# An encoder layer in float32 on one core: up products in twos, a first group of three, diagonals without a split, and smaller stores at the end

## The chip, the cores and the metric

The kernel runs on one core of a Trainium2 chip. A core has a matrix engine (TensorE, PE in the profile, with its weight loads shown as PEld), a vector engine (VectorE, DVE), an activation engine (ScalarE, ACT), a general engine (GpSimd, POOL), and a sync engine (SyncE, SP) whose queue issues most of the transfers; 16 DMA engines carry them. Each engine runs its own instructions in order and waits on semaphores for the others. The metric is the device time of one execution in microseconds (us); the time of a kernel is the median of its runs.

## The reference

One layer of an encoder, on 512 tokens of 2048 channels, all in float32 and with one output:

```python
xn = rms_norm(x, attn_norm_g)
u_val, u_gate, q, k, v = split(xn @ w_in)            # 2048 -> 5 x 1024
y_conv = silu(layer_norm(dwconv31(u_val * sigmoid(u_gate))))
y_na = neighbourhood_attention(q, k, v, rpb)         # 16 heads of 64, 8x64 grid
mixed = concat(rms_norm(y_conv), rms_norm(y_na))
x = x + mixed @ w_out                                # 2048 -> 2048
xn = rms_norm(x, ffn_norm_g)
gate, val = split(dwconv3(xn @ w_up))                # 2048 -> 2 x 5632
x = x + (silu(gate) * val) @ w_down                  # 5632 -> 2048
out = rms_norm(x, final_norm_g)
```

A root-mean-square norm divides each token's vector by the root of its mean square. The factor belongs to a token, so it may be applied after a product with the weights; the kernel does that.

## The kernel before

**Data.** Activations lie transposed: a tile has 128 channels as partitions and the 512 tokens as columns. Weights come from memory in units of 128 x 1024 (512 KB) into a ring of 7 buffers named `raw`.

**Products of float32 made of parts.** Each weight unit is split in two by `parts` (L113-118): ACT makes the rounded part `whi` (L116), DVE the remainder `wlo` (L117); each has 4 buffers. Activations are split likewise. `mm3` (L124-129) adds three matmuls to a bank of PSUM: high by high (L127), high by low (L128), low by high (L129). The list `plan` holds the units in order; `weights()` hands out the next one and makes units up to 3 ahead (`AHEAD`).

**Order.** The kernel is written against a tile framework that orders the instructions of an engine by its own estimate of when they are due, within the data dependences, so that work stands elsewhere in an engine's queue than the source's order says. Work beside the main loop is written as generators in the lists `steps` and `asteps`; `tick` (called after each product) runs one step of the first generator of each and ties what it issues behind the last matmul of that product. A `yield` in such a generator so puts off its rest by one product.

**The per-token factor.** `rsqrt_steps` (L179-213) makes 1/sqrt(mean + eps) for each token. With the sum of squares over channels in `acc`, matmuls with a column of ones (L190) put the tokens on the partitions, 128 x 4 values; L192 and `root` (L172-177: a square root on ACT, then a reciprocal and one correction step on DVE) work on those. To get the factor back as a row per token and the same on every partition, the kernel makes diagonal matrices of it and multiplies them by ones: the 128 x 4 factor is split into a rounded part (L197) and the rest (L198), each is spread on four diagonals side by side (`dg`, 128 x 512, L202), and two matmuls (L208) add them up; ACT copies the result from PSUM (L212). It is called six times: for the norm before the input projection (about 45 us into the span), for the layer norm of the convolution, for the two group norms (the convolution's, `ra`, near 497 us), for the norm before the feed-forward part (`rstd2`, near 683 to 694 us) and for the final one (`rstd3`, near 2010 us).

**The output projection** is made in two halves of 16 products; its first half begins before `ra` exists, and `read_a` then takes each bank with L586 (product by `ra`) and L587 (sum into `x2`). Its banks come from `psm`, a pool of three banks of PSUM with the tag "mm".

**The feed-forward part.** The up product is made with seven products instead of eight half-size ones (a scheme of Strassen's kind). For each of the 44 values of f (128 gate and 128 value channels) `factors` (L655-681) forms the seven weight units out of four loaded ones by sums on DVE (L666, L668, L673, L677), and `combine` and `halves` (L597-635) have formed the seven combinations of activations once, each of 256 columns and split (L600 on ACT, L601 on DVE), laid side by side as one 512-column tile: high in the left half, low in the right.

`up` (from f = 4, L708-769) makes a product c of eight channel tiles k: a *wide* matmul (L716) takes `whi` by both halves of the tile, 512 columns; a *low* one (L721) takes `wlo` by the left half, 256 columns, and adds to the bank's right half. A product is seven wide, eight low, and the last wide. After it ACT copies the bank's halves out (`vv`, `pl`, L728), and DVE sums the seven results into gate and value.

`up_apart` (f = 0 to 3, L771-809) works with three 256-column matmuls per k (`mm3`) and banks of 256 columns, copied by L800 and L803. For f = 0, `first_two` (L789) interleaves the first two products: both run their first seven k and then their last, since the last tile of the combinations comes late.

The product c = 6 has the bank "po", all others take the three "mm" banks in turn.

`hidden` (L821) applies the token factor, the convolution of width 3 and the gate; `down` (L836) multiplies four hidden tiles by the down weights (`pd`), ACT copies the bank (L847), and POOL issues a DMA that adds it to the residual in memory (L848). The down products of one group of four f run between the up products of the next (`between`).

**The tail.** The last down products and the final norm: 384 tokens are handled by channel, 128 by token. `finish` (L902) scales a pair of 128 x 384 tiles, on DVE (L912) or for every third pair on ACT and POOL (L909, L910), and stores the pair by one DMA (L916); the first pair is stored by two DMAs of one tile each (L914). `spread` (L933) runs between the last matmuls and calls the second half of `rsqrt_steps` at the step (g, k) = (1, 1), then one `finish` at each later step. Stores go by SP's queue, in order. The last token block follows with four stores (L975).

Of the kernel before, what the change touches and what calls it, by code (L numbers as in the profile page):

```python
# [67 lines left out]
def layer(ctx: ExitStack, tc: tile.TileContext, xT, xG, w_in, w_v, w_out, w_up, w_down, par, tab, g3, out, last_out):  # L68
# [110 lines left out]
    def rsqrt_steps(acc, n, name, to=slice(0, S), keep=True, by_token=None, free=False, rest=1):  # L179

        def bank():
            if free:
                return psa.tile([P, 2, S], F32, tag="sc", name="st")[:, 0]
            return psa.tile([P, S], F32, tag="po", name="st")

        m = (to.stop - to.start) // P
        ps = bank()[:, :m]
        v, r, y = (sm.tile([P, S // P], F32, tag="rs" + c, name="rs" + c)[:, :m] for c in "vry")
        for i in range(m):
            nc.tensor.matmul(ps[:, i:i + 1], acc[:, to.start + i * P:to.start + (i + 1) * P], ones[:, 0:1],  # L190
                             start=True, stop=True)
        nc.vector.tensor_scalar(v, ps, 1.0 / n, EPS, op0=ALU.mult, op1=ALU.add)  # L192
        root(r, y, v)
        if by_token is not None:
            by_token.append(y)
        yh, yl = (sm.tile([P, S // P], dt, tag="rs" + c, name="rs" + c)[:, :m] for c, dt in (("h", F32R), ("l", F32)))
        nc.vector.tensor_copy(yh, y)  # L197
        nc.vector.tensor_sub(yl, y, yh.bitcast(F32))  # L198
        ds = []
        for part in (yh.bitcast(F32), yl):  # L200
            ds.append(t2("dg", F32R)[:, :m * P])
            nc.vector.tensor_mul(ds[-1].rearrange("p (i k) -> p i k", k=P), ident.unsqueeze(1).broadcast_to([P, m, P]),  # L202
                                 part.unsqueeze(2).broadcast_to([P, m, P]))
        for _ in range(rest):
            yield
        ps = bank()[:, :m * P]
        for i, dg in enumerate(ds):
            nc.tensor.matmul(ps, ones_r, dg, start=i == 0, stop=i == 1)  # L208
        if not keep:
            return ps  # L210
        res = t2(name)
        nc.scalar.activation(res, ps, AF.Copy)  # L212
        return res
# [431 lines left out]
    def stats2():  # L645
        acc2, q = t2("acc2"), t2("sq")
        nc.sync.dma_start(acc2, sq2[0])
        nc.sync.dma_start(q, sq2[1])
        yield
        nc.vector.tensor_add(acc2, acc2, q)  # L650
        yield
        yield
        rstd2.append((yield from rsqrt_steps(acc2, D, "rstd2", free=True, rest=2)))
# [53 lines left out]

    def up(f, between):  # L708

        def product(c):  # L710

            w = weights()
            ps = (psa.tile([P, S], F32, tag="po", name="pu") if c == 6 else
                  psm.tile([P, S], F32, tag="mm", name="pu"))
            def wide(k):
                return nc.tensor.matmul(ps, w[0][:, k * P:(k + 1) * P], comb[c][k], start=k == 0, stop=k == U - 1)  # L716

            for k in range(U - 1):
                wide(k)
            for k in range(U):  # L720
                nc.tensor.matmul(ps[:, H:], w[1][:, k * P:(k + 1) * P], comb[c][k][:, :H], start=False, stop=False)  # L721
            i = wide(U - 1)
            tick(i)
            between(c)
            return ps[:, :H], ps[:, H:]

        def copy(to, ps):
            nc.scalar.activation(to, ps, AF.Copy)  # L728

        def pair(name):  # L730
            return t2(name).rearrange("p (i t) -> p i t", i=2)

        def both(x):
            return x.unsqueeze(1).broadcast_to([P, 2, H])


        vv, low = pair("vv"), pair("pl")
        for i in range(2):
            m, l = product(i)
            copy(vv[:, i], m)  # L740
            copy(low[:, i], l)
        m7, l = product(2)
        add(vv, vv, low)
        low = pair("pl")
        copy(low[:, 0], l)
        m1, l = product(3)
        copy(low[:, 1], l)
        uu, v = pair("uu"), pair("vl")
        u, u2 = uu[:, 0], uu[:, 1]
        add(u2, m7, low[:, 0])  # L750
        add(v, vv, both(u2))
        m6, l = product(4)
        add(u, m1, low[:, 1])
        low = pair("pl")
        copy(low[:, 0], l)
        add(u2, u, m6)
        m2, l = product(5)
        add(u2, u2, low[:, 0])
        add(v, v, both(u2))
        add(vv[:, 1], vv[:, 1], u2)  # L760
        low, g = pair("pl"), pair("g")
        copy(low[:, 0], l)
        add(g[:, 0], u, m2)
        m3, l = product(6)
        copy(low[:, 1], l)
        add(g[:, 1], vv[:, 1], m3)
        add(g, g, low)
        g, v = (t.rearrange("p i t -> p (i t)") for t in (g, v))
        return g, v

    def up_apart(f, between):  # L771

        def begin(c):
            return weights(), (psa.tile([P, S], F32, tag="po", name="pu") if c == 6 else
                               psm.tile([P, S], F32, tag="mm", name="pu"))[:, :H]

        def part(c, w, ps, ks):
            for k in ks:
                m = comb[c][k]
                i = mm3(ps, w, k, m[:, :H], m[:, H:], k == 0, k == U - 1)  # L780
            return i

        def product(c):
            w, ps = begin(c)
            tick(part(c, w, ps, range(U)))
            between(c)
            return ps

        def first_two():  # L789
            got = [begin(c) for c in range(2)]  # L790
            for c in range(2):
                tick(part(c, *got[c], range(U - 1)))
            for c in range(2):
                part(c, *got[c], range(U - 1, U))
            return [ps for _, ps in got]

        vv, v, uu, g = (t2(n).rearrange("p (i t) -> p i t", i=2) for n in ("vv", "vl", "uu", "g"))
        both = lambda x: x.unsqueeze(1).broadcast_to([P, 2, H])
        for i, ps in enumerate(first_two() if f == 0 else map(product, range(2))):
            nc.scalar.activation(vv[:, i], ps, AF.Copy)  # L800
        u, u2 = uu[:, 0], uu[:, 1]
        add(v, vv, both(product(2)))
        nc.scalar.activation(u, product(3), AF.Copy)  # L803
        add(u2, u, product(4))
        add(v, v, both(u2))
        add(vv[:, 1], vv[:, 1], u2)
        add(g[:, 0], u, product(5))
        add(g[:, 1], vv[:, 1], product(6))
        return tuple(t.rearrange("p i t -> p (i t)") for t in (g, v))
# [123 lines left out]
    def spread(g, k):  # L933
        if (g, k) == (0, 1):
            next(stats)
        elif (g, k) == (1, 1):
            try:
                next(stats)
            except StopIteration as e:
# [3 lines left out]
            nc.scalar.activation(rb[1], rb[0], AF.Copy)  # L943
        elif rb and pairs:
            at = pairs.pop(0)
            finish(at, rb[at % 3 == 1], at % 3 == 1)

    for g, ps in enumerate(banks):
        for i in range(CH):
# [100 lines left out]
```

## Time and profile before

| | |
|---|---|
| median of 3 runs | 2035.49 us (2032.01 to 2036.54) |
| the profiled execution | 2032.23 us |
| its span, first to last instruction | 2030.3 us |
| PE busy | 2016.6 us, 99% of the span |
| DVE, ACT, POOL busy | 1673.5, 1045.7, 159.7 us |
| mean granted TensorE clock | 0.998 of full speed |
| DMA | 276.4 MB, 136 GB/s on average |

The rows shown below are of these kinds. A row of the busy times has an engine, its busy time, the share of the span and the count of instructions. The chain is the work that ended last, followed back: start (us), length (us), engine, name of the result and line. A group's row has line, engine, operation, result and operands, shapes, count, then busy time and the mean of one (ns), then the idle time of the engine ahead of it and what ended it. A row of PE's waits has the waiting matmul, what released it, and total, count and longest wait in us. A timeline row has start, length, engine and line, with neighbours of one kind merged (x2); a matmul's length there covers its whole way through the engine, and the distance of two starts is what one costs. A row of GB/s gives the DMA rate in 40 equal slices of its window.

### The profile page before, as it was taken

What the parts mean: (1) busy time and instruction counts of PE and PEld (TensorE: products, weight loads), DVE (VectorE), ACT (ScalarE), POOL (GpSimd) and SP (SyncE); (2) the same over time, 40 slices, a digit from 0 to 9 for tenths busy, and PEclk for the clock granted to TensorE, in tenths of its full rate; (3) what the DMA queues carried; (4) which work ended last, traced back from release to release, by engine and by line L of the source; (5) the groups of instructions that cost most, each with busy time, mean ns of one, the idle gap of its engine ahead of it and who ended that gap; (6) DMA issues with size and microseconds to landing.
All of it is one profiled execution on the core that took longest, in us unless ns stands there. A gap on an engine that the chain in (4) does not pass through costs nothing.

```text
span 2030.3 us, 28220 instructions
## 1 busy us (share of the span) xinstructions
PE 2016.6 (99%) x10672; PEld 1726.0 (85%) x10672; DVE 1673.5 (82%) x2293; ACT 1045.7 (52%) x1674; POOL 159.7 (8%) x188
## 2 busy tenths in 40 slices
PE   9999999999999999999999999999999999999998
PEld 7888888888888998888888888888888888888887
DVE  7986888988577898888888888788888888889875
ACT  7323344466346555554555555555555555555563
POOL 0000000000001001111111111111111111110111
PEclk9999999999999999999999999999999999999999
DMA  7232333346347436566565565555565565564583
GB/s 256 83 104 86 115 96 109 104 131 212 104 124 177 124 105 145 127 144 146 125 146 146 135 136 146 134 136 145 125 145 146 125 146 145 130 141 126 145 212 120
DMA packets 97207, 276.40 MB, mean 136 GB/s; under 512 B 10928, under 2 KB 11696, under 8 KB 97072
## 3 DMA queue, kind: packets, MB, share of 16 engines
q1 hardware_dynamic: 71712, 228.45, 36.6%
q0 software_dynamic: 25216, 46.15, 15.4%
q8 instruction: 84, 1.38, 0.3%
q14 instruction: 51, 0.42, 0.1%
q10 hardware_dynamic: 144, 0.01, 0.0%
HBM read 220.04 MB, written 54.53 MB: 135 GB/s over the span
## 4 chain that ended last, share of the span: by engine, by line
PE 97%; DVE 2%; issue 0%; ACT 0%; DMA 0%; ACTq 0%; DVEq 0%
PE pu L716 25%; PE pu L721 13%; PE pd L129 8%; PE pd L127 8%; PE pd L128 8%; PE pj L127 6%; PE pj L129 5%; PE pj L128 5%; PE po L127 3%; PE po L128 3%; PE po L129 3%; PE pv L313 1%; PE pv L315 1%; PE pv L314 1%; PE pu L127 1%; PE pu L128 1%
## 5 line engine op out<-in xcount | busy, mean ns | idle before, releaser
L116 ACT ACTIVATE whi<-raw 128x1024 fp32r<-128x1024 f32 x364 | 384.8, 1058 | 481.8 <-PE pj L128 137.2
L117 DVE TENSOR_TENSOR wlo<-raw,whi 128x1024 fp32r<-128x1024 f32 x364 | 444.5, 1222 | 206.6 <-ACT whi L116 194.7
L716 PE MATMUL pu<-xc,whi 128*128 128x512 f32 x2240 | 574.5, 391 | 0.0
L716 PEld LDWEIGHTS pu<-xc,whi 128*128 128x128 f32 x2240 | 409.1, 189 | 73.7
L721 PEld LDWEIGHTS pu<-xc,wlo 128*128 128x128 f32 x2240 | 305.6, 190 | 21.9
L721 PE MATMUL pu<-xc,wlo 128*128 128x256 f32 x2240 | 312.3, 282 | 0.0
L128 PE MATMUL pd<-hl,whi 128*128 128x512 f32 x640 | 249.2, 389 | 0.0
L129 PE MATMUL pd<-hh,wlo 128*128 128x512 f32 x640 | 249.2, 391 | 0.0
L127 PE MATMUL pd<-hh,whi 128*128 128x512 f32 x640 | 249.0, 391 | 0.0
L848 POOL DMA_DIRECT2D x2d<-pdc x160 | 139.6, 874 | 1165.4 <-ACT pdc L847 952.4
L128 PE MATMUL pj<-xl,whi 128*128 128x512 f32 x512 | 200.1, 391 | 0.0
L129 PE MATMUL pj<-xh,wlo 128*128 128x512 f32 x512 | 199.8, 390 | 0.0
L127 PE MATMUL pj<-xh,whi 128*128 128x512 f32 x512 | 198.8, 393 | 0.0
L728 ACT ACTIVATE pl<-pu 128x256 f32<-128x256 f32 x280 | 104.5, 382 | 165.4 <-PE pu L716 165.2
L116 ACT ACTIVATE whi<-ws 128x1024 fp32r<-128x1024 f32 x132 | 139.8, 1059 | 80.0 <-PE pu L716 57.8
L117 DVE TENSOR_TENSOR wlo<-ws,whi 128x1024 fp32r<-128x1024 f32 x132 | 161.0, 1220 | 20.1 <-ACT whi L116 20.0
L367 DVE SCALAR_TENSOR_TENSOR y<-ch,prm,y 128x500 f32<-128x500 f32 (+14 forms) x240 | 173.5, 742 | 4.3
L129 PEld LDWEIGHTS pd<-hh,wlo 128*128 128x128 f32 x640 | 120.1, 188 | 28.8 <-DVE wlo L117 3.0
L128 PEld LDWEIGHTS pd<-hl,whi 128*128 128x128 f32 x640 | 120.3, 188 | 24.9
L127 PEld LDWEIGHTS pd<-hh,whi 128*128 128x128 f32 x640 | 120.5, 188 | 21.9
L847 ACT ACTIVATE pdc<-pd 128x512 f32<-128x512 f32 x160 | 93.8, 588 | 84.2 <-PE pd L129 84.1
L127 PEld LDWEIGHTS pj<-xh,whi 128*128 128x128 f32 x512 | 96.2, 188 | 20.4 <-issue 0.2
(206 smaller groups left out, 2887.3 us busy)
## 6 DMA issues: line engine op xcount, KB each, us to landing
raw<-in_w_up SPq DMA_DIRECT2D x176, 512.0 KB, 3.7
raw<-in_w_down SPq DMA_DIRECT2D x88, 512.0 KB, 4.0
x2d<-pdc POOLq DMA_DIRECT2D x160, 256.0 KB, 4.9
raw<-in_w_in SPq DMA_DIRECT2D x60, 512.0 KB, 3.8
raw<-in_w_out SPq DMA_DIRECT2D x32, 512.0 KB, 3.7
raw<-in_w_v SPq DMA_DIRECT2D x16, 512.0 KB, 4.1
tab<-in_tab SPq DMA_DIRECT2D x32, 256.0 KB, 5.0
x<-in_xG SPq DMA_DIRECT2D x16, 256.0 KB, 5.4
```

What stands on the lines that cost most here:

```text
L116: i = nc.scalar.activation(hi[:, :n], raw[:, :n], AF.Copy)
L117: j = nc.vector.tensor_sub(lo[:, :n], raw[:, :n], hi[:, :n].bitcast(F32))
L127: nc.tensor.matmul(ps, hi[:, a], mh, start=start, stop=False)
L128: nc.tensor.matmul(ps, hi[:, a], ml, start=False, stop=False)
L129: return nc.tensor.matmul(ps, lo[:, a], mh, start=False, stop=stop)
L313: nc.tensor.matmul(ps, xh, wh[:, f], start=kk == 0, stop=False)
L367: nc.vector.scalar_tensor_tensor(y[:, a:b], h[:, a + j - PAD:b + j - PAD], prm[:, o + j:o + j + 1], y[:, a:b], op0=ALU.mult, op1=ALU.add)
L716: return nc.tensor.matmul(ps, w[0][:, k * P:(k + 1) * P], comb[c][k], start=k == 0, stop=k == U - 1)
L721: nc.tensor.matmul(ps[:, H:], w[1][:, k * P:(k + 1) * P], comb[c][k][:, :H], start=False, stop=False)
L728: nc.scalar.activation(to, ps, AF.Copy)
L847: nc.scalar.activation(t, ps, AF.Copy)
L848: nc.gpsimd.dma_start(xd[d], t, accum_op=ALU.add)
```

## The change

It has four parts. *Diagonals*: in `rsqrt_steps` the cast, the subtraction and the spreading of the rest are replaced: the first diagonal (in the rounded type) is made from the factor itself, and the second, for each 128 columns, as identity times factor less the first diagonal, by one operation. *Twos*: in `up` the products (0,1), (2,3) and (4,5) share one block of low matmuls: eight wide of the first, one wide of the second (on its own bank), eight low of the first, eight low of the second, seven wide of the second. *Threes*: for f = 0 the first three products are interleaved, and `stats2` waits one product longer. *Stores*: `spread` takes up the factor one step earlier, and all pairs that DVE finishes are stored by two DMAs of one tile each.

```diff
@@ rsqrt_steps
-        yh, yl = (sm.tile([P, S // P], dt, tag="rs" + c, name="rs" + c)[:, :m] for c, dt in (("h", F32R), ("l", F32)))
-        nc.vector.tensor_copy(yh, y)
-        nc.vector.tensor_sub(yl, y, yh.bitcast(F32))
-        ds = []
-        for part in (yh.bitcast(F32), yl):
-            ds.append(t2("dg", F32R)[:, :m * P])
-            nc.vector.tensor_mul(ds[-1].rearrange("p (i k) -> p i k", k=P), ident.unsqueeze(1).broadcast_to([P, m, P]),
-                                 part.unsqueeze(2).broadcast_to([P, m, P]))
+        ds = [t2("dg", F32R)[:, :m * P] for _ in range(2)]
+        nc.vector.tensor_mul(ds[0].rearrange("p (i k) -> p i k", k=P), ident.unsqueeze(1).broadcast_to([P, m, P]),
+                             y.unsqueeze(2).broadcast_to([P, m, P]))
+        for i in range(m):
+            o = slice(i * P, (i + 1) * P)
+            nc.vector.scalar_tensor_tensor(ds[1][:, o], ident, y[:, i:i + 1], ds[0][:, o].bitcast(F32),
+                                           op0=ALU.mult, op1=ALU.subtract)
@@ stats2
         yield
+        yield
         nc.vector.tensor_add(acc2, acc2, q)
@@ up
+        opened = {}
+
+        def bank(c):
+            return (psa.tile([P, S], F32, tag="po", name="pu") if c == 6 else
+                    psm.tile([P, S], F32, tag="mm", name="pu"))
+
+        def wides(c, w, ps, ks, stop=False):
+            for k in ks:
+                i = nc.tensor.matmul(ps, w[0][:, k * P:(k + 1) * P], comb[c][k], start=k == 0,
+                                     stop=stop and k == ks[-1])
+            return i
+
+        def lows(c, w, ps, stop=False):
+            for k in range(U):
+                i = nc.tensor.matmul(ps[:, H:], w[1][:, k * P:(k + 1) * P], comb[c][k][:, :H], start=False,
+                                     stop=stop and k == U - 1)
+            return i
+
         def product(c):
             w = weights()
-            ps = (psa.tile([P, S], F32, tag="po", name="pu") if c == 6 else
-                  psm.tile([P, S], F32, tag="mm", name="pu"))
-            def wide(k):
-                return nc.tensor.matmul(ps, w[0][:, k * P:(k + 1) * P], comb[c][k], start=k == 0, stop=k == U - 1)
-
-            for k in range(U - 1):
-                wide(k)
-            for k in range(U):
-                nc.tensor.matmul(ps[:, H:], w[1][:, k * P:(k + 1) * P], comb[c][k][:, :H], start=False, stop=False)
-            i = wide(U - 1)
+            if c == 6:
+                ps = bank(c)
+                wides(c, w, ps, range(U - 1))
+                lows(c, w, ps)
+                i = wides(c, w, ps, range(U - 1, U), stop=True)
+            elif c % 2:
+                ps = opened.pop(c)
+                lows(c, w, ps)
+                i = wides(c, w, ps, range(1, U), stop=True)
+            else:
+                ps, opened[c + 1] = bank(c), bank(c + 1)
+                wides(c, w, ps, range(U))
+                wides(c + 1, made[weights.at], opened[c + 1], range(1))
+                i = lows(c, w, ps, stop=True)
             tick(i)
@@ up_apart
-        def first_two():
-            got = [begin(c) for c in range(2)]
-            for c in range(2):
+        def first_three():
+            got = [begin(c) for c in range(3)]
+            for c in range(3):
                 tick(part(c, *got[c], range(U - 1)))
-            for c in range(2):
+            for c in range(3):
                 part(c, *got[c], range(U - 1, U))
             return [ps for _, ps in got]
...
-        for i, ps in enumerate(first_two() if f == 0 else map(product, range(2))):
-            nc.scalar.activation(vv[:, i], ps, AF.Copy)
+        early = iter(first_three() if f == 0 else map(product, range(3)))
+        for i in range(2):
+            nc.scalar.activation(vv[:, i], next(early), AF.Copy)
         u, u2 = uu[:, 0], uu[:, 1]
-        add(v, vv, both(product(2)))
+        add(v, vv, both(next(early)))
@@ spread
-        elif (g, k) == (1, 1):
+        elif (g, k) == (1, 0):
...
-            finish(at, rb[at % 3 == 1], at % 3 == 1)
+            finish(at, rb[at % 3 == 1], at % 3 == 1, at % 3 != 1)
```

## The prediction

> **What bounds the kernel now.** I read first the busy times and the chain of work that ended last, then the waits of TensorE (PE), then the chain and the timeline at each place that the change touches.
>
> ```profile
> PE 2016.6 (99%) x10672; PEld 1726.0 (85%) x10672; DVE 1673.5 (82%) x2293; ACT 1045.7 (52%) x1674; POOL 159.7 (8%) x188
> PE 97%; DVE 2%; issue 0%; ACT 0%; DMA 0%; ACTq 0%; DVEq 0%
> L716 PE MATMUL pu<-xc,whi 128*128 128x512 f32 x2240 | 574.5, 391 | 0.0
> L721 PE MATMUL pu<-xc,wlo 128*128 128x256 f32 x2240 | 312.3, 282 | 0.0
> ```
> ```profile
> PE idle L237 <- DVE warm L234: 1.6, 1, 1.6
> PE st L208 <- DVE dg L202: 1.5, 1, 1.5
> PE pu L127 <- ACT xc L600: 0.8, 1, 0.8
> PE st L190 <- DVE acc L170: 0.3, 1, 0.3
> ```
>
> PE is busy for 99% of the span and makes 97% of the chain. In 2030 us it waits for data in four places, 4.2 us in all; two of them (L208, L600) lie at the start of the feed-forward part. So a change can gain in three ways only: by those two waits, by closer matmuls, and in the last 10 us, where the stores set the end. It can lose by any new wait of PE. The number of matmuls stays.
>
> **Up products in twos.** The chain shows how closely the matmuls of `up` follow one another:
>
> ```profile
> 1197.38 1.59 PE pu L716 x7
> 1198.97 0.95 PE pu L721 x8
> 1199.92 1.84 PE pu L716 x8
> 1201.76 0.95 PE pu L721 x8
> ```
> ```profile
> 753.69 0.12 PE pu L127
> 753.81 0.12 PE pu L128
> ```
>
> Seven wide matmuls behind a block of `pd` take 1.59 us, 0.227 each; eight would take 1.817. Behind a low block eight take 1.84: some 0.024 more. A low block takes 0.95 against 8 x 0.12 = 0.96 by the steady 256-column matmuls of `up_apart`: a little less. So a product of 1.84 + 0.95 = 2.79 stands over 1.817 + 0.96 = 2.777 by 0.013 to 0.024 (the rows are rounded to 0.01); I take 0.018. That is the price of going from wide to low and back. In twos, a pair makes one such round where it made two. By the order of the changed program there are 179 rounds instead of 280: of the 120 pairs, 101 run their sixteen low matmuls in one block, while in 19 (mostly products 2 and 3 of a function number f with f%4 = 0 or 3) the scheduler puts the second product's wide matmuls in among the down products. 101 x 0.018 = **-1.8 us**; bounds -2.4 (0.024 each) and 0.
>
> A page of the Trainium skill speaks against this term: "TensorE: Matmul & The Clock Gate", section on the back-to-back issue gap, has a gap that depends on a matmul's own columns, beside a weight load that is pipelined with it. By that, the order of wide and low is indifferent and the term is 0; the excess behind a low block in the rows above disagrees with it. This is rival B.
>
> What the pairs cost: the second product's `wlo` is wanted seven wide matmuls (1.6 us) earlier. No up product of the steady part waits for a part in the list of waits above, and the scheduler has put the parts in the same order on DVE, so I charge nothing; if the cover were gone, each late `wlo` costs up to one DVE operation, 1.2 us. Two banks of `psm` are held at once, so product c+1 must find its bank free one wide matmul after product c's eight; that is rival C.
>
> **First f in threes.** In the first f PE stops twice:
>
> ```profile
> 674.82 0.42 ACT xc L600
> 675.29 0.39 PE pu L127
> ```
> ```profile
> 682.86 0.16 DVE L192 TENSOR_SCALAR rsv<-st 128x4 f32<-128x4 f32 x1
> 689.15 0.16 DVE L177 SCALAR_TENSOR_TENSOR rsy<-rsy,rsr 128x4 f32<-128x4 f32 x1
> 690.77 0.17 DVE L197 CAST rsh<-rsy 128x4 fp32r<-128x4 f32 x1
> 690.84 1.22 DVE L666 TENSOR_TENSOR ws<-raw 128x1024 f32<-128x1024 f32 x1
> 691.98 0.16 DVE L198 TENSOR_TENSOR rsl<-rsy,rsh 128x4 f32<-128x4 f32 x1
> 692.05 0.69 DVE L202 TENSOR_TENSOR dg<-ident,rsh 128x512 fp32r<-128x512 f32 x1
> ```
> ```profile
> 691.15 0.28 PE L129 MATMUL pu<-xc,wlo 128*128 128x256 f32 x1
> 692.88 0.47 PE L208 MATMUL st<-dg,ones 128*128 128x512 f32 x1 [1.45 <-DVE dg L202]
> ```
>
> The first stop (0.8 in the list of waits, 0.9 with the restart) is for the eighth `xc`. In the changed order the third product's 21 matmuls stand there: 21 x 0.12 = 2.5 us of work, and `xc` at 675.24 is due 1.7 us before they end. Gain 0.9. The second stop is 1.61 us from the end of the last matmul at 691.27 to L208, and about 0.2 more for the restart: 1.8. Its cause is the small operations of the root, which stand between 1.2 us operations on DVE (L177 at 689.15, L197 only at 690.77, L198 at 691.98). In the change the square-sum waits one step longer (second `yield`), the cast L197 and the subtraction L198 are gone, and the diagonal's multiplication stands behind fewer weight operations; stepping the changed DVE order through with the durations above I get the diagonal at about 692.1, and PE there at 691.9: 0 to 0.2 is left. Both stops together: -2.8 + 0.1 = -2.7.
>
> Against this stands a new wait. Three banks are open at once, so product 3 takes product 0's bank and must wait until ACT has copied it (L800). On ACT this copy now stands behind two `whi` (products 4 and 5):
>
> ```profile
> 676.98 1.05 ACT L116 ACTIVATE whi<-ws 128x1024 fp32r<-128x1024 f32 x1
> 677.93 0.63 ACT L800 ACTIVATE vv<-pu 128x256 f32<-128x256 f32 x2
> 678.46 1.05 ACT L116 ACTIVATE whi<-raw 128x1024 fp32r<-128x1024 f32 x1
> ```
>
> `whi` of product 4 can begin when product 0's last matmul has released its buffer, about 677.2; two at 1.0 take it to 679.2, the copy (0.36) to 679.5. PE has done the three products at 677.9: it stood still from 674.4 (675.29 less 0.9), and 2.5 and nine closing matmuls at 0.12 follow. New wait 1.65. Net **-1.0 us**; bounds -2.7 (the copy goes ahead of the second `whi` and more) and +0.2 (the diagonal comes one 1.2 us operation later).
>
> **The diagonals without a split.** Four 128-column operations with a subtraction (three in the tail) replace the cast, the subtraction and one multiplication; the trace has no 128x128 operation of this kind, so each lies between the 0.16 of a 128x4 one and the 0.42 of a 128x256 one; I take 0.25, being nearer in size to the latter's half. Removed 0.17 + 0.16 + 0.69 = 1.02, added 4 x 0.25 = 1.0 (0.64 to 1.68). The sum is the same, but the first diagonal comes 0.3 earlier and the second at 0.7 to 1.7 behind the first's issue, instead of 0.6. At four of six places the result has slack or follows PE. Two do not:
>
> ```profile
> 45.98 0.42 PE st L208
> ```
> ```profile
> 497.49 0.64 PE L208 MATMUL st<-dg,ones 128*128 128x512 f32 x2
> 500.26 0.39 PE L127 MATMUL po<-mah,whi 128*128 128x512 f32 x1
> ```
> ```profile
> 498.27 0.58 ACT L212 ACTIVATE ra<-st 128x512 f32<-128x512 f32 x1
> ```
> ```profile
> 498.69 0.69 DVE L170 TENSOR_TENSOR accna<-accna,sq 128x512 f32<-128x512 f32 x1
> 499.29 1.28 DVE L586 TENSOR_TENSOR oa<-po,ra 128x512 f32<-128x512 f32 x2
> ```
>
> At 46 us the first diagonal's matmul holds the chain 0.42 where a matmul takes 0.23: the gap goes, **-0.1** (0 to -0.2). At 497 us the scheduler now puts the pair of `ra` five matmuls later: 5 x 0.227 = 1.13. The fourth product of the output projection (500.26) needs the bank that the first L586 reads. Before, that read ended at about 499.98, 0.28 before it was needed; after it would begin when the copy L212 ends (498.85 + 1.13 = 499.98), end at 500.7, and PE stops until 500.74: **+0.5** (0 to +0.6, the copy may start sooner behind the pair).
>
> **The tail.** The last 10 us are the stores':
>
> ```profile
> 2014.91 0.87 SPq L914 DMA_DIRECT2D out_T<-fin  x2
> 2018.03 5.28 SPq L916 DMA_DIRECT2D out_T<-fin  x7
> ```
> ```profile
> 2016.01 4.93 POOL L910 TENSOR_TENSOR fin<-x,rb 128x384 f32<-128x384 f32 x5 [39.02 <-ACT rb L943]
> ```
> ```profile
> GB/s 0 0 0 0 0 104 406 369 425 378 397 407 378 406 425 369 416 397 378 406 397 397 416 369 416 397 388 363 391 378 372 372 403 372 397 208 0 0 0 0
> ```
> ```profile
> GB/s 0 0 0 0 0 0 0 0 0 0 0 0 108 369 338 353 369 369 384 369 353 399 338 169 16 0 0 0 0 0 0 0 0 0 0 0 0 0 0 0
> ```
>
> The first row of rates is 2017 to 2030: from the first whole-pair store on, about 393 GB/s without a break. Between the first pair's halves (second row, 2014.5 to 2018.5, about 364 GB/s) and that the queues are empty for about two microseconds, since the sync engine waits with pair 1 for POOL. In the changed order one half of pair 2 (196.6 KB) stands ahead of pair 1 and fills the hole: 196.6 KB / 393 = -0.5. The other seven halves go at the halves' rate: 7 x 196.6 KB x (1/364 - 1/393) = +0.28. The four added issues lie beside the transfers. Net **-0.2** (-0.5 to +0.3). The earlier `spread` moves the diagonal's matmuls by no matmul that PE waits for.
>
> "DMA: Bandwidth & Descriptors" of the Trainium skill, section on specifications, lets every descriptor of 512 B and more run at line rate; by it the halves lose nothing and the tail gains 0.5. The two rows of rates, 364 and 393, disagree.
>
> **Sum.** -1.8 - 1.0 - 0.1 + 0.5 - 0.2 = -2.6 us. The profiled execution (2032.23, span 2030.3) lies 3.3 under the median of the three runs, 2035.49, and inside their spread; the sum is taken from the median: **2032.9 us**. What a measurement tells from no change is 0.2%, 4.1 us.
>
> **The rivals.** A is this forecast. B: the pairs save nothing, the excess belonging to each product; for it speaks only that 0.018 is less than two digits of the rows; -0.8, 2034.7. C, slower: in the ten groups f = 8, 12, ... product 3's bank is the one of product 0, whose two copies (0.38 each, as are all `L728`) now stand on ACT behind `whi` of product 5 (1.06) and the hidden tile's 512-column copy (nearest row `pdc`, 0.59): 1.06 + 0.59 + 2 x 0.38 = 2.4 us after product 2's wide block.
>
> ```profile
> L728 ACT ACTIVATE pl<-pu 128x256 f32<-128x256 f32 x280 | 104.5, 382 | 165.4 <-PE pu L716 165.2
> L847 ACT ACTIVATE pdc<-pd 128x512 f32<-128x512 f32 x160 | 93.8, 588 | 84.2 <-PE pd L129 84.1
> ```
>
> The scheduler has a low block and ten or eleven `pd` matmuls there (0.95 + 2.3 = 3.2 us), so it should be covered by 0.8; where it isn't, each group costs up to 2.4. The sum turns to slower from (4.1 + 2.6)/10 = 0.67 us a group; at 1 us a group the time is 2042.9. D, faster: product 3's new wait is short or absent and no wait at 500 us appears: -2.6 - 1.65 - 0.5 = -4.8, 2030.7. That the change doesn't do what it says is counted in the 19 pairs.
>
> **How the numbers follow.** A 0.50, B 0.12, C 0.10, D 0.28. D gives faster, with a fifth of A, whose bounds (2.4 for the pairs, 0.5 for the tail) reach -4.1: 0.28 + 0.08 = 0.36. C gives slower: 0.10. Same: 0.54. The range leaves out D's far end and C beyond a slight wait: from 2035.49 - 6.5 = 2029.0 to 2035.49 + 1.0 = 2036.5.
>
> **What would show it.** Right: low blocks of sixteen at 0.12 each and one long interval less a pair; the wait on `xc` gone from the list of PE's waits, L208's under 0.3, a new one of about 1.6 for L800; one of 0.4 or so at 500 us for L586; DMA busy without a hole from 2015. Wrong: PE waits in the groups of four between 850 and 1900 us, or steady wide matmuls over 0.227.

## The result, and the profile after

The changed kernel takes 2029.9 us (median of 22 runs, 2029.43 to 2033.16) against 2032.7 us for the kernel before on the same chips (22 runs). The ratio, here and below that of the mean times, is 0.9983, 95% interval 0.9976 to 0.9989. It is faster by some 3 us, between 2.2 and 4.9: clear of no change, but inside the 4.1 us within which the prediction counts a time as the same. The prediction was 2.6 us less, and as a time 2032.9 us.

The profiled execution took 2030.16 us with a span of 2028.4 (before 2032.23 and 2030.3). The busy times and the chain by engine, from the page of the changed kernel, and PE's waits (waiting matmul, releaser, total, count, longest in us):

```profile
PE 2015.4 (99%) x10672; PEld 1726.5 (85%) x10672; DVE 1675.5 (83%) x2298; ACT 1050.9 (52%) x1674; POOL 159.5 (8%) x188
PE 96%; DVE 2%; DMA 1%; ACT 0%; issue 0%; SPq 0%; ACTq 0%; DVEq 0%
L718 PE MATMUL pu<-xc,whi 128*128 128x512 f32 x2240 | 552.9, 391 | 0.0
L724 PE MATMUL pu<-xc,wlo 128*128 128x256 f32 x2240 | 296.6, 283 | 0.0
```
```profile
PE idle L236 <- DVE warm L233: 1.6, 1, 1.6
PE pu L127 <- ACT vv L823: 1.5, 1, 1.5
PE st L190 <- DVE acc L170: 0.3, 1, 0.3
PE po L127 <- DVE oa L585: 0.3, 1, 0.3
```

The two waits of the first f (L208 for the diagonal, 1.5; L127 for the last `xc`, 0.8) are gone from the list. Two new ones stand in it: product 3 for the copy of product 0's bank (L823), and the fourth product of the output projection for L585. Both were in the prediction.

Where the time went, stage by stage. The stages are cut at the starts of matmuls in the two timelines:

| stage | before, us | after, us | difference |
|---|---|---|---|
| start to the first up matmul | 669.22 | 670.29 | +1.07 |
| f = 0 and 1 | 44.35 | 43.71 | -0.64 |
| f = 2 to the first down matmul | 48.71 | 48.68 | -0.03 |
| the next 192 down matmuls and what runs between them | 121.94 | 121.89 | -0.05 |
| to the tail's first matmul | 1080.85 | 1079.01 | -1.84 |
| to PE's last matmul | 55.75 | 55.74 | -0.01 |
| to the end of the span | 9.51 | 9.07 | -0.44 |
| sum | 2030.33 | 2028.39 | -1.94 |

Of the +1.07 in the first stage, 0.64 is there already at the first matmul of the value projection, which lies at 52 us. That start moves by itself: kernels whose code is the same up to there had it at these times (timelines of the kernel before, of the one with twos alone, and of the one with the stores alone; these kernels are described below). The last row is the changed kernel's:

```profile
51.94 0.39 PE L313 MATMUL pv<-whi,xh 128*128 128x512 f32 x1
```
```profile
52.54 0.39 PE L313 MATMUL pv<-whi,xh 128*128 128x512 f32 x1
```
```profile
53.05 0.39 PE L313 MATMUL pv<-whi,xh 128*128 128x512 f32 x1
```
```profile
52.59 0.39 PE L312 MATMUL pv<-whi,xh 128*128 128x512 f32 x1
```

Without the 0.64 the two spans differ by 2.58 us. For changes of this size the stages of a profile tell more than the times, whose 95% intervals are 2.6 to 5.3 us wide here; the verdicts below rest on stages, and the times are given beside them. Each kernel has one profile, so a stage is one reading: in four kernels with the same code in f = 0 and 1 that stage took 44.31 to 44.53 us, while the stage behind it agrees within 0.04 in all of these.

### The profile page after: what moved, and what is told of

Read it like the earlier page. It is cut to its first block, busy times and chain, and to the rows that moved or that the text cites. A ratio compares the mean times of both kernels' runs of the same rounds, so it can differ in the third digit from the quotient of the medians.

```text
span 2028.4 us, 28313 instructions
## 1 busy us (share of the span) xinstructions
PE 2015.4 (99%) x10672; PEld 1726.5 (85%) x10672; DVE 1675.5 (83%) x2298; ACT 1050.9 (52%) x1674; POOL 159.5 (8%) x188
## 4 chain that ended last, share of the span: by engine, by line
PE 96%; DVE 2%; DMA 1%; ACT 0%; issue 0%; SPq 0%; ACTq 0%; DVEq 0%
PE pu L718 25%; PE pu L724 13%; PE pd L129 8%; PE pd L127 8%; PE pd L128 8%; PE pj L127 5%; PE pj L128 5%; PE pj L129 5%; PE po L127 3%; PE po L128 2%; PE po L129 2%; PE pv L313 1%; PE pv L312 1%; PE pv L314 1%; PE pu L127 1%; PE pu L129 1%
## 5 line engine op out<-in xcount | busy, mean ns | idle before, releaser
L718 PE MATMUL pu<-xc,whi 128*128 128x512 f32 x2240 | 552.9, 391 | 0.0
L724 PEld LDWEIGHTS pu<-xc,wlo 128*128 128x128 f32 x2240 | 292.3, 191 | 13.9
L724 PE MATMUL pu<-xc,wlo 128*128 128x256 f32 x2240 | 296.6, 283 | 0.0
L127 PE MATMUL pd<-hh,whi 128*128 128x512 f32 x640 | 249.6, 390 | 0.0
L127 PE MATMUL pj<-xh,whi 128*128 128x512 f32 x512 | 198.9, 393 | 0.0
L127 PEld LDWEIGHTS pd<-hh,whi 128*128 128x128 f32 x640 | 120.4, 188 | 22.6
L127 PEld LDWEIGHTS pj<-xh,whi 128*128 128x128 f32 x512 | 96.3, 188 | 20.7 <-ACT xh L249 0.2
```

The lines of the kernel that those rows point to most:

```text
L127: nc.tensor.matmul(ps, hi[:, a], mh, start=start, stop=False)
L718: i = nc.tensor.matmul(ps, w[0][:, k * P:(k + 1) * P], comb[c][k], start=k == 0, stop=stop and k == ks[-1])
L724: i = nc.tensor.matmul(ps[:, H:], w[1][:, k * P:(k + 1) * P], comb[c][k][:, :H], start=False, stop=stop and k == U - 1)
```

## The experiments

### Each part alone

Four kernels, each the kernel before with one part of the change: the products in twos; the first three products interleaved, with the second `yield`; the diagonals; the single-tile stores with the earlier `spread`. The edits are those of the diff above.

> The kernel before with only the up products in twos. Theory (a round from wide to low and back costs 0.018 us; 101 rounds fewer): the span from the first pd matmul to the last shortens by 1.8 to 1.9 us, nothing else moves, and the time falls by about 1.9 us. Rival B (the excess belongs to the product, not to the transition): 0. Rival C (product 3 waits for product 0's bank in ten groups): PE shows waits on the copy of L728's kind between 850 and 1900 us.

Measured: ratio 0.9987 (0.9979 to 0.9996). The next 192 down matmuls 121.74 and the stage after them 1079.05 us: -0.20 and -1.80, together -2.0, all other stages within 0.05 (the start apart). The trace has 179 low blocks, 101 of them of sixteen matmuls, where the kernel before has 280 of eight. No wait is added to PE's list. 2.0 / 101 is 0.0198 us a round. Rival B and rival C fall.

> The kernel before with only the first three products interleaved and the second yield. Theory: the wait on xc at 674 us (0.92 and 0.10 of restart) goes, a wait of 1.7 us for product 0's copy comes before product 3, and the wait for the diagonal falls from 1.6 to about 0.6, since the cast, the subtraction and a weight sum still stand ahead of it: net -0.3 us in the first f. Rival (the interleaving alone is what pays): -1.0 us or more.

Measured: ratio 1.0007 (0.9998 to 1.0016). f = 0 and 1 take 44.49 us, +0.14, and the stage with the first down matmuls 122.40, +0.46 (0.41 of it in four new gaps of 0.1 us between 763 and 767). The waits for `xc` and for the diagonal are gone from PE's list, and this one is in it:

```profile
PE pu L127 <- ACT vv L802: 2.2, 1, 2.2
```

A miss by 0.9 us, and on the side that I had not set down: the interleaving alone loses. The +0.14 is inside what this stage does by itself; the +0.46 is not, since the same stage takes 121.94 or 121.95 us in the kernel before and in those with the diagonals or the stores alone. The wait for the copy was 2.4 with what the profile doesn't count as idle, not 1.7, and the diagonal still cost 0.3, less than the 0.6 expected. Product 3 began at 680.72 us here and at 680.61 in the changed kernel, though the first up matmul began 0.6 us sooner (669.70 against 670.29): what releases it keeps its own time. That led to the third group of runs.

> The kernel before with only the diagonals made without a split. Theory: at 500 us PE waits 0.4 for L585's read and restarts in 0.1 (+0.5); at 46 us -0.1; at 691 us the first diagonal no longer stands behind the weight sum and its wait falls from 1.6 to about 0.2, but the second now does, with four operations of 0.35, and PE waits about 1.1 for it: net about +0.2 us in all. Rival (shorter work on DVE pays by itself): -1.4 us.

Measured: ratio 1.0003 (0.9994 to 1.0012). At 500 us the wait for L585 stands as expected (0.42 of idle time and 0.11 behind the next matmul), at 46 us the 0.20 lost around the first diagonal's matmul is gone but 0.17 is lost around the second's, and PE's list has:

```profile
PE pu L127 <- ACT xc L599: 0.8, 1, 0.8
PE pu L127 <- ACT uu L802: 0.7, 1, 0.7
PE po L127 <- DVE oa L585: 0.3, 1, 0.3
PE st L207 <- DVE dg L197: 0.2, 1, 0.2
```

The wait for the first diagonal fell to 0.33 and 0.90 us of idle time came after it: f = 0 and 1 took 44.16, -0.19. What PE waits for there is the copy of product 3 (L802), not the second diagonal that I had named. The size was right, the cause of the second wait was not. Alone the diagonals are no gain.

> The kernel before with only the single-tile stores and the earlier spread. Theory: one tile's store fills part of the hole in the transfers after the first pair (-0.5) and the smaller packets cost 0.3 elsewhere: -0.2 to -0.4 us between PE's last matmul and the end of the span. Rival (the rate does not depend on the packet here): -0.5 us and no slice of the rate below 380 GB/s once the queue is full. Rival (order of the queue was no limit): 0 or +0.3.

Measured: ratio 0.9997 (0.9988 to 1.0006); from PE's last matmul to the end 9.05 us, -0.46. The same 9.03 to 9.07 is in all kernels below that have these stores.

The parts alone add to -2.0 + 0.6 + 0.3 - 0.45 = -1.5 us, together they gave -2.6. The 1 us between lies mostly at two places. Some 0.6 of it is in the first two f, where the wait for the copy is 1.69 us from matmul to matmul instead of the 2.39 of the interleaving alone, and some 0.3 at 763 us, where one gap of 0.1 stands in place of four.

### More rounds

```diff
-            for k in range(U - 1):
+            for k in range(U // 2 - 1):
                 wide(k)
             for k in range(U):
+                if k == U // 2:
+                    for j in range(U // 2 - 1, U - 1):
+                        wide(j)
                 nc.tensor.matmul(ps[:, H:], w[1][:, k * P:(k + 1) * P], comb[c][k][:, :H], start=False, stop=False)
```

> The kernel before with each low block of eight cut into two of four, four wide matmuls between: 560 rounds instead of 280, the same matmuls. Theory (a round costs 0.018 to 0.020 us, most of it in the first four wide intervals): 280 rounds more, +4.2 to +5.6 us, spread evenly over the steady part, the other stages as before. Rival B (no price of the round): 0.

Measured: ratio 1.0026 (1.0017 to 1.0035). The two stages of the steady part take 122.43 and 1085.18 us, +0.49 and +4.33: 4.82 / 280 = 0.0172 us a round. The chain of the changed kernel, and then of this one:

```profile
1197.24 2.04 PE pu L718 x9
1199.28 1.91 PE pu L724 x16
1201.20 3.20 PE pu L718 x14
```
```profile
1199.56 0.68 PE pu L716 x3
1200.24 0.47 PE pu L724 x4
1200.71 0.93 PE pu L716 x4
1201.64 0.47 PE pu L724 x4
1202.11 0.93 PE pu L716 x4
```

Sixteen low matmuls in a row take 1.91 (0.119 each). Four wide ones behind four low ones take 0.93 where four at 0.227 would take 0.908. So the first wide matmuls behind a low block are the slow ones, fewer rounds gain and more rounds lose at nearly the same price. The starts of the matmuls in the changed kernel's trace give it position by position: the first five intervals behind a low block average 0.233, 0.236, 0.228, 0.233 and 0.231 us against 0.2267 from the sixth on, and the first two low ones 0.113 and 0.119 against 0.120; that is +0.027 and -0.007, or 0.020 a round. A gap that depends on a matmul's own columns, beside a pipelined weight load, as "TensorE: Matmul & The Clock Gate" of the Trainium skill has it (section on the back-to-back issue gap), gives 0 for both kernels; the runs give -2.0 and +4.8. Why the chip behaves so is not shown.

### What product 3 waits for

Three kernels on top of the changed one: product 2 of the first f in a bank of its own, so that product 3 needs no copy (`bank`); `RA_AFTER = 1` in place of 2, so that the two matmuls of `ra` come 112 and 103 matmuls sooner (`ra`), not the some 90 that I had expected; both.

```diff
-            got = [begin(c) for c in range(3)]
+            got = [begin(c) for c in range(2)]
+            got.append((weights(), psa.tile([P, S], F32, tag="tr", name="pu", bufs=2)[:, :H]))
```

> The changed kernel with product 2 of the first f in a bank of the tag tr, so that product 3 finds a free bank without product 0's copy. Theory: the wait of 1.69 us at 679 us and its restart go; since the scheduler then puts the diagonal's matmul 38 matmuls later, no new wait takes their place, and the 0.2 at the diagonal goes too: -1.7 to -2.0 us against the changed kernel in the first f. Rival (the next late thing takes the place: the weight part of product 3 or 4, or the diagonal): -0.5 us or less.

Measured: ratio 0.9995 (0.9986 to 1.0004), and by the span without its start 1.75 us slower than the changed kernel. The wait of 1.5 at 679 us is gone, and this is PE's list:

```profile
PE pd L129 <- DVE wlo L117: 1.4, 1, 1.4
PE pu L127 <- ACT vv L824: 0.9, 1, 0.9
PE st L207 <- DVE dg L201: 0.4, 1, 0.4
```

After its first two f the kernel is 0.15 us ahead of the changed one (43.56), and at the first down matmuls, 763 us, it loses 1.5 us to a `wlo` that stands behind two of the `hl` operations in DVE's queue, where in the changed kernel it stands ahead of them (123.61 for that stage, +1.72). The rival holds: taken away, the wait came back in three other places and cost more.

> The changed kernel with one step less ahead of the factor ra, so that its two matmuls stand some 90 matmuls earlier. Theory: the wait at 500.6 us (0.42 and 0.11 of restart), which comes from ra's late place, goes: -0.5 us against the changed kernel between 480 and 560 us. Rival (the work of the attention that then stands behind it on DVE is late instead): 0.

Measured: ratio 0.9987 (0.9978 to 0.9995). The wait for L585 is gone and the first up matmul begins 0.42 us sooner (0.66, less 0.23 by the start). The first two f then take 44.41 instead of 43.71, so that nothing is left. Weight sum L668 on DVE and product 3's first matmul on PE, in the changed kernel:

```profile
673.36 1.22 DVE L668 TENSOR_TENSOR raw<-raw 128x1024 f32<-128x1024 f32 x1 [0.78 <-DMA raw<-in_w_up]
```
```profile
680.61 0.39 PE L127 MATMUL pu<-xc,whi 128*128 128x256 f32 x1 [1.53 <-ACT vv L823]
```

and in the kernel with the earlier `ra`:

```profile
673.45 1.23 DVE L668 TENSOR_TENSOR raw<-raw 128x1024 f32<-128x1024 f32 x1 [1.53 <-DMA raw<-in_w_up]
```
```profile
680.65 0.39 PE L127 MATMUL pu<-xc,whi 128*128 128x256 f32 x1 [2.23 <-ACT vv L823]
```

PE came sooner and product 3 did not. L668 is a sum for the second f. It waits for its transfer, and the last combinations, which the first f needs, stand behind it on DVE; behind these on ACT follow `xc`, two `whi`, and the copy that product 3 waits for. ACT in the changed kernel, and then in this one:

```profile
677.63 0.71 ACT L599 ACTIVATE xc<-b 128x256 fp32r<-128x256 f32 x2
678.28 1.06 ACT L116 ACTIVATE whi<-ws 128x1024 fp32r<-128x1024 f32 x1
```
```profile
677.73 0.71 ACT L599 ACTIVATE xc<-b 128x256 fp32r<-128x256 f32 x2
678.35 1.04 ACT L116 ACTIVATE whi<-ws 128x1024 fp32r<-128x1024 f32 x1
```

In both, `whi` starts right behind the last `xc`.

> The changed kernel with both of these edits. Theory: the two gains add, -2.2 to -2.5 us against the changed kernel, some -5 us against the kernel before. Rival (one hides the other): -1.7 or less.

Measured: ratio 0.9996 (0.9987 to 1.0005): the loss of `bank` remains (PE waits 1.4, 0.7 and 0.6 us for `wlo`, a copy and the diagonal), the gains do not add.

To test that chain, the sum of the second f was tied behind the last combination, with the earlier `ra` and without the extra bank:

```diff
                 load(A11)
-                add(a[A21], a[A21], a[A11])
+                if f == 1:
+                    with tc.issue_after(lastc[-1].ins):
+                        add(a[A21], a[A21], a[A11])
+                else:
+                    add(a[A21], a[A21], a[A11])
```

(`lastc` holds the subtractions L600; in the other kernels the load is an operand of the sum.)

> The kernel with the earlier ra, and the weight sum L668 of the second f tied behind the last combination on DVE, ahead of which it stood waiting for its transfer. Theory (with the earlier ra the first f began 0.66 us sooner and won nothing, because the combinations stood behind that sum, which waits for a transfer that PE's earlier start does not move): the wait of 2.2 us before product 3 falls to about 1.7 and the 0.5 us of the earlier ra is kept at the end of the first f. Rival (product 0's copy is bound by its weight part's buffer, as I had reckoned): the wait stays at 2.2.

Measured: ratio 0.9983 (0.9974 to 0.9991), 2029.45 us. Product 3's first matmul:

```profile
679.78 0.39 PE L127 MATMUL pu<-xc,whi 128*128 128x256 f32 x1 [1.53 <-ACT vv L828]
```

and the `whi` ahead of that copy on ACT, which now waits for PE:

```profile
674.96 0.71 ACT L599 ACTIVATE xc<-b 128x256 fp32r<-128x256 f32 x2
677.45 1.06 ACT L116 ACTIVATE whi<-ws 128x1024 fp32r<-128x1024 f32 x1 [1.79 <-PE pu L128]
```

The wait is back at 1.5, the first two f take 43.71 and the earlier `ra` is kept. So with the order as it was, two things bound that copy almost together: the chain through L668's transfer, and the release of product 0's weight buffer, which I had reckoned with. The release comes 7.99 us behind the first up matmul here (669.46); 7.99 behind the changed kernel's 670.29 is 678.28, the very time at which its `whi` starts. This kernel is 0.4 to 0.5 us ahead of the changed one by its stages; the times (2029.45 and 2029.9, the same ratio to the kernel before) don't tell them apart.

### DVE's load

From 682 to 767 us DVE is busy for 82 of 85 us in the kernel before and in the changed one, so its load could be why a removed wait returned elsewhere. With both edits, two of the four weight sums of the first four f were given to GpSimd, in a second kernel with the sum tied as above:

```diff
+        more = nc.gpsimd.tensor_add if f < CH else add
...
-                add(a["s"], a["s"], a[A11])
+                more(a["s"], a["s"], a[A11])
...
-                add(a["s"], a["s"], a[A12])
+                more(a["s"], a["s"], a[A12])
```

> The kernel with both edits (product 2's own bank, earlier ra), and the sums L673 and L677 of the first four f made by GpSimd, eight operations of 1.22 us less for DVE, which is busy for 96% of the stretch from 682 to 767 us. Theory (DVE's load is what turns each wait that is removed there into the next one): the waits at 695 to 701 us (0.6 and 0.7) and at 763 us (1.5) go: about -2.5 us against the kernel with both edits, about -1.5 against the changed kernel. Rival (the order of DVE's queue alone): the waits stay, or GpSimd's sums, which by its 1.02 us for 384 columns take some 2.7 us, come late and PE waits for a whi: 0 or slower.

Measured: ratio 1.0056 (1.0043 to 1.0069), 2044.67 us: a loss of 13 us against the kernel with both edits. The sums on GpSimd by lines, and two stretches of POOL and DVE:

```profile
L677 POOL TENSOR_TENSOR ws<-ws,raw 128x1024 f32<-128x1024 f32 x4 | 16.3, 4066 | 35.4 <-DVE wlo L117 35.4
L673 POOL TENSOR_TENSOR ws<-ws,raw 128x1024 f32<-128x1024 f32 x4 | 11.6, 2904 | 25.5 <-DVE wlo L117 19.1 <-DVE rsy L176 6.4
```
```profile
682.65 3.31 POOL L677 TENSOR_TENSOR ws<-ws,raw 128x1024 f32<-128x1024 f32 x1 [9.95 <-DVE wlo L117]
692.40 3.31 POOL L673 TENSOR_TENSOR ws<-ws,raw 128x1024 f32<-128x1024 f32 x1 [6.43 <-DVE rsy L176]
```
```profile
683.62 2.89 DVE L650 TENSOR_TENSOR acc<-acc,sq 128x512 f32<-128x512 f32 x1
```
```profile
692.26 1.23 DVE L666 TENSOR_TENSOR ws<-raw 128x1024 f32<-128x1024 f32 x1
693.40 2.33 DVE L177 SCALAR_TENSOR_TENSOR rsy<-rsy,rsr 128x4 f32<-128x4 f32 x1
```

A 128x512 sum on DVE takes 0.69 and a 128x4 operation 0.16; here they take 2.89 and 2.33, and end within 0.6 us of the end of POOL's operation (685.96, 695.71). Of the eight sums on GpSimd, six took 2.7 to 3.3 us, and each met one DVE operation that took 1.9 to 2.3 us longer than elsewhere, 12.9 us together; during the other two DVE ran as usual, and they took 5.05 us. So the sums that were to relieve DVE, of 8 x 1.22 = 9.8 us, held it up for longer.

A part of the loss is PE's granted clock. In the kernel with both edits it is 1.00 in all these stretches; here it falls twice behind PE's waits, of 3.7 us for the diagonal up to 697.6 and of 1.0 and 2.1 us up to 775.8. In the rows below (`--windows`) the stretch, its length and the busy times of PE, its weight loads, DVE, ACT and POOL come first, then the clock, the DMA share and the GB/s:

```profile
698.10:701.40 3.30, 3.30 (x16) 3.20 (x16) 3.15 (x8) 0.60 (x1) 0.00 (x0) 0.50 0.45 155
776.60:779.90 3.30, 3.30 (x12) 2.75 (x11) 3.30 (x5) 1.09 (x5) 0.00 (x0) 0.50 0.57 159
```

Half the clock for twice 3.3 us is some 3.3 us of the 13 (an estimate from these rows).

> The kernel of the run before (GpSimd's sums) with the weight sum of the second f tied behind the combinations as well. Theory: the last activation tile comes about 1.4 us earlier, and what still waits for product 0's or 1's copy in the first f shrinks: 0 to -0.7 us against it. Rival: no wait there is left to shrink: 0.

Measured: ratio 1.0040 (1.0028 to 1.0053), 2041.51 us: -3.2 against the run before, where at most -0.7 was expected. The wait for `xc` (1.9 us, new in the kernel with GpSimd's sums) is gone, and 1.6 us at the first down matmuls. No shorter wait is behind the latter: the two waits there are the same, 1.0 and 2.1 us, but the granted clock behind them is 1.00 where it was 0.50, and why is not shown. In the first f it is 0.50 for longer than in the run before, from 694.3 to 701.0 us. Since GpSimd's sums delayed DVE itself, these two runs don't say whether DVE's load or only the order of its queue makes the wait wander. That stays open.

### The stores

```diff
-            finish(at, rb[at % 3 == 1], at % 3 == 1, at % 3 != 1)
+            finish(at, rb[at % 3 == 1], at % 3 == 1, at == 2)
```

> The changed kernel, with single-tile stores kept for the first and the third pair (pair 2, the one that fills the hole) alone. Theory of the prediction (filling the hole gains 0.5, smaller packets cost 0.3): the time from PE's last matmul to the end of the span falls by 0.2 to 0.3 us against the changed kernel's 9.07. Rival (smaller packets cost nothing): it stays at 9.07. Rival (the single tiles also help by being issued sooner): it rises toward 9.5.

Measured: ratio 0.9988 (0.9979 to 0.9997); from PE's last matmul to the end 8.98 us, against 9.07 in the changed kernel and 9.51 before. The DMA rate of the changed kernel from 2012 to 2031 us and of this one:

```profile
GB/s 0 0 0 0 68 365 369 26 252 162 0 272 407 353 369 362 385 401 372 366 372 369 369 411 401 352 392 397 367 392 371 112 0 0 0 0 0 0 0 0
```
```profile
GB/s 0 0 0 3 352 362 110 162 252 0 181 401 359 391 388 414 395 414 388 382 395 414 395 407 356 380 392 380 380 367 13 0 0 0 0 0 0 0 0 0
```

Filling a part of the hole gives 0.53 (one slice of 0 GB/s is left in both rows), and six more single tiles cost 0.09, where the prediction's rates gave 0.24 for six. The earlier `spread` moved nothing by itself: the first store is issued 5.91 us ahead of the end of PE's last matmul in the kernel before and in the changed one. One reservation: the kernels with threes alone and with the diagonals alone, whose tails have the stores of the kernel before, took 10.06 and 10.02 us there, with the last four stores landing 3.9 and 3.8 us after their issue instead of 3.2, while the kernel before, the twos and the rounds took 9.49 to 9.51. I found no cause; the gain of 0.44 is against the lower of the two.

## Why the prediction was right

The sum was -2.6, the profile without its start gives -2.58 and the times some -3 (2.2 to 4.9). That it fits to a few hundredths is luck: the first f and the place at 46 us came out 0.5 us worse than forecast, the pairs and the tail 0.3 to 0.4 better. The forecast time, 2032.9, was 3.0 us too high. It was taken from the median of three runs, 2035.49, which lies 2.8 above the 2032.7 of 22 runs; the measured 2029.9 is 0.9 above the range's lower end. Term by term:

- **Pairs**, predicted -1.8 (0 to -2.4): -2.0 with the twos alone, -1.9 in the changed kernel, where a new gap of 0.1 at 764 us is in the same stages. The price of a round, 0.018 by the chain's rows, is 0.020 by taking rounds away and 0.017 by adding them. The 101 rounds counted from the program's order are those that ran. Rival B, at 0.12, was refuted by both kernels.
- **The first f**, predicted -1.0: -0.64. The two waits that go were sized well: 0.92 + 0.10 and 1.61 + 0.08 = 2.7 (the prediction's own 0.9 and 1.8 also make 2.7, where it writes 2.8). The new wait was 1.69, against 1.65 reckoned. Left out were its restart (0.10) and that of the diagonal's matmul (0.08), and the diagonal came 0.2 late, the upper end of what I had left. The cause of the new wait was half seen. I put it to the release of product 0's buffer at 677.2, and the trace has that `whi` start at 678.28, which is 677.2 plus the 1.07 of the later start. With the sum tied, where only the release is left, the wait is the same, so the reckoned cause suffices. But `whi` also stands right behind the last `xc` copy on ACT, a chain that the prediction did not see; that it ends no later than the release in the changed kernel is luck, and with PE 0.4 to 0.6 us sooner (the earlier `ra`, the interleaving alone) it set the wait.
- **`ra`**, predicted +0.5: +0.5 (0.42 and 0.11). But as a term of the sum it was not free-standing: with it taken away alone, the first f waited 0.7 longer, and nothing was gained.
- **46 us**, predicted -0.1: 0, the end of its bounds. The 0.20 around the first diagonal's matmul went and 0.17 came around the second's; from the eighth matmul ahead of the first diagonal's to the value projection both kernels take 7.98 us. One of the four operations that replace the split takes 0.346 us, not 0.25, within the bounds given.
- **The tail**, predicted -0.2: -0.44. What filled the hole was worth what was reckoned, though the sign of no hole from 2015 us did not come; the price of smaller packets was mis-sized, 0.1 instead of 0.28. The rate of 364 GB/s came from the first pair's two stores, which stand alone in the queue; with the queue full the single tiles lose little. The rule of "DMA: Bandwidth & Descriptors" of the Trainium skill (section on specifications), with no loss at these sizes, was nearer than that row.
- **Rival C** (0.10): PE waits nowhere between 850 and 1900 us for a copy. **Rival D** (0.28): both new waits came. By the prediction's bound of 4.1 us the outcome is the same time, to which it gave 0.54.

## What to carry to other kernels

Price a reordering of the busiest engine by the rows of its chain (blocks of the same kind, behind different neighbours): 0.02 us a round, too small for any list of waits, was the largest term here. Where an engine is nearly always busy beside the critical one, don't count a removed wait as gained until the next late thing is known: an edit that took 1.7 us of waiting away made the kernel 1.75 us slower. And before adding up savings ahead of a stage, look for a chain there that doesn't begin with the engine you are speeding up, such as a transfer whose consumer stands in an in-order queue ahead of urgent work.

## What the runs showed of the hardware

- A wide matmul's interval is longer for the first five behind narrower ones: 0.228 to 0.236 us where the steady ones take 0.2267, and a change of width and back costs 0.017 to 0.020 us.
- A GpSimd sum of two 128x1024 float32 tiles took 2.7 to 5.05 us beside a busy DVE, against 1.22 on DVE. During six of the eight, one DVE operation was held until about when the sum ended (0.16 became 2.33, 0.69 became 2.89); during the two of 5.05 us none was. The Trainium skill, "GPSIMD Engine Reference", section on specifications, names the shared access to SBUF, with contention for DVE instructions with two inputs from there; the held operations have two such inputs, but so have some that ran as usual beside the two sums of 5.05 us.
- In the two kernels with GpSimd's sums PE waited 3.7 us near 694 us and 1.0 and 2.1 us near 774. Behind these waits the granted clock was 0.50, for 3.3 us at both places in one kernel and for 6.7 us at the first place alone in the other.
- Transfers of 192 KB single tiles ran nearly as fast as 384 KB pairs once the queue was full (0.09 us for six; the tails with the changed kernel's stores took 9.03 to 9.07 us, the one with four single tiles 8.98), and slower (about 364 against 393 GB/s) when only two were under way.
